# Retention's gates stored as products, with their silu in retention's stage, and attention's blocks begun less often in the first third of the gates

## The chip, the cores and the metric

The kernel runs on one core of one Trainium2 chip. The core has TensorE (PE in the profile, PEld for its weight loads), VectorE (DVE), ScalarE (ACT), GpSimd (POOL) and SyncE (SP), which here only issues transfers. Each engine takes its instructions in order from a queue of its own and waits on semaphores. The metric is the device time of one execution in microseconds, as the median of several runs. The time before is 2192.56 us, the median of three runs from 2191.86 to 2193.46.

## The reference

One decoder block on x of 1024 rows by 1024 columns, in float32. One input projection of the normalised rows feeds two mixers and the gates that merge them:

```
xn = rmsnorm(x, norm1_g)
qa, ka, va, qr, kr, vr, gr, gate_a, gate_b = columns of xn @ w_in
o_a = dilated sliding-window attention (12 heads, 3 dilations), mixed by softmax denominators
o_r = head_groupnorm(retention(qr, kr, vr)) * silu(gr)
y   = sigmoid(gate_a) * (o_a @ w_proj_a) + sigmoid(gate_b) * (o_r @ w_proj_b)
x   = x + y @ w_out
x   = x + square(relu(rmsnorm(x, norm2_g) @ w_up)) @ w_down
```

The change concerns `silu(gr)`, where silu(v) = v * sigmoid(v) and gr has 1024 rows by 2048 columns (4 heads of 512), and the time at which the pieces of attention are worked on.

## The kernel before

Every large product is done in three passes: each operand is split into a high and a low part (`split`, L369 on ScalarE and L372 on VectorE), and TensorE multiplies high by high, high by low and low by high (`Pipe.group`, L273). Weights come from memory into `raw` tiles, are split into `wh` and `wl` in six buffers, and are used (`Weights`).

TensorE's order is written out by hand. Its unit is a *slot* of `Pipe.step`: one group of matmuls, with other work put between the terms of the group if it is due in that slot (`Pipe.at(lag, ...)`). The order of the other engines and of the transfers is made by a planner, which goes by its own costs for instructions and transfers and gives earlier instructions of the program precedence; some orders are pinned (`keep_in_program_order`).

The stages that the change touches:

- **The gates' stage** (L871 on): 24 units of 7 slots, 168 slots, as a Strassen product (7 products of quarters instead of 8; `product`). Units 0 to 7 are the merge gates, `NG`; units 8 to 15 are retention's queries and keys, `NQ`; units 16 to 23 are retention's own gates `gr`. Each unit gives four results of 128x512: two come straight from PSUM (after N2 and N4), two from SBUF tiles `u2` and `u3` that VectorE has summed (L450, L455). `result` sends them out: the merge gates through a sigmoid (`gate_out`, L746, L747) into `sg_d`; queries and keys into `rqk_d`, copied first where they are in PSUM (L885); retention's gates through a sigmoid (L881) and a product with themselves (L882) into `sr_d`. The last two units' results go out on GpSimd's queue, the others on SyncE's (L886, L887). The pools `sg` and `u2`, `u3` have two buffers each.
- **Attention** runs in between: 96 blocks of 128 queries. Block n begins in slot `begins(n)` of this stage, with three pieces: `scores` in that slot (L814 on TensorE, L817 and L819 on VectorE, an exponential L820 on ScalarE), `turn` two slots later (L826 on TensorE, L828 on VectorE) and `values` four slots later (L833 on TensorE, a copy L835 on ScalarE, and for each second block a store). Each piece takes one of the two PSUM buffers `tr`. Loads of queries, keys and values (L786 to L788) are issued from SyncE ahead of the blocks.
- **The mix** of attention's three head groups, eight times (`combine`): loads 7 and 19 slots after the beginning of the last block of a head slot, arithmetic from 12 and 24 slots after it, with an exponential on ScalarE (L490), products on VectorE (L502, L504), transposes on TensorE (L510). Once the last block is done, `close_heads` frees attention's memory for more weight buffers.
- **Values for retention** (56 more slots of token units, L718 to L737), which still hold the last mix.
- **Retention** (L1129 on), over 32 items, a head and a chunk of 128 rows each, with the two output projections of the mixers as filler for TensorE. Item m is normalised (`output`), and two iterations later `turn_o` transposes it (L1118), scales and shifts it (L1122, Identity with a scale and a bias, four times 128x128 on ScalarE), multiplies it on VectorE by the gates in tile `sr` (L1124; loaded at L1030, two buffers) and splits it into the operand of a projection. Between them stand the splits of the state (`prepare`, tiles `Sh`, `Sl`).

Of the kernel before, what the change touches and what calls it, by code (L numbers as in the profile page):

```python
# [10 lines left out]
F = mybir.dt.float32  # L11
R = mybir.dt.float32r
AF = mybir.ActivationFunctionType
OP = mybir.AluOpType
PSUM = bass.MemoryType.PSUM
DRAM = bass.MemoryType.DRAM

P = 128
# [287 lines left out]
def strassen_order(units):  # L306


    order = [(0, "N1"), (1, "N1"), (0, "N2"), (1, "N2")]
    for j in range(units):  # L310
        late = j + 3 >= units
        order += [(j, "N6"), (j, "N5")] + ([] if late else [(j + 2, "N1")]) + [(j, "N7")]
        order += [(j, "N3")]
        order += [(j + 2, "N2")] if not late else [(units - 1, ("N1", "N2")[j + 3 - units])] if j + 1 < units else []
        order += [(j, "N4")]
    return order
# [3 lines left out]
def hybrid_block(ctx: ExitStack, tc: tile.TileContext, a: dict, out: bass.AP):  # L320
    nc = tc.nc
# [46 lines left out]
    def split(dst_h, dst_l, src, pinned=False):  # L368
        hi = nc.scalar.activation(dst_h, src, AF.Copy)  # L369
        if pinned:  # L370
            tc.keep_in_program_order(hi)
        nc.vector.tensor_tensor(dst_l, src, dst_h.bitcast(F), op=OP.subtract)  # L372
# [25 lines left out]
    NG, NQ = KT, 2 * RH  # L398
# [18 lines left out]
    pipe = Pipe(nc)  # L417

    def product(tag, j, name, unit, operands, pu, result):

        u = unit.setdefault(j, {})
        bank = BANK[name]
        fresh = bank not in u
        if fresh:
            u[bank] = mm.tile([P, 512], F, name="mm")
        piece, half = OPERAND[name]
        wh, wl = W[tag, j, piece]
        xh, xl = operands[name]
        terms = []
        for k in range(4):  # L430
            o = 512 * half + k * P
            terms.append((wh[:, o:o + P], wl[:, o:o + P], xh[:, k, :], xl[:, k, :]))
        pipe.step(u[bank], terms, None, fresh)
        ps = u[bank]
        lo, hi = halves()
        if name == "N1":
            u["b"] = ms.tile([P, 512], F, name="ms")
            nc.scalar.activation(u["b"], ps, AF.Copy, scale=-1.0)
        elif name == "N2":
            result(j, 0, lo, ps)  # L440
        elif name == "N6":
            u["u2"] = pu().tile([P, 512], F, name="u2")
            nc.scalar.activation(u["u2"], ps, AF.Copy)
        elif name == "N5":
            u["u3"] = pu().tile([P, 512], F, name="u3")
            nc.scalar.activation(u["u3"], ps, AF.Copy)
            if j == 0:
                W.free((tag, "first"))
        elif name == "N7":
            nc.vector.tensor_tensor(u["u3"], ps, u["u3"], op=OP.subtract)  # L450
            result(j, 1, hi, u["u3"])
        elif name == "N4":
            result(j, 1, lo, ps)
        elif name == "N3":
            nc.vector.tensor_tensor(u["u2"], ps, u["u2"], op=OP.subtract)  # L455
            result(j, 0, hi, u["u2"])
        if name in ("N2", "N7", "N4", "N3"):
            W.free((tag, j, piece))
# [58 lines left out]
    def mix_next():  # L517

        if mixing:
            mixing.pop(0)()  # L520
            if len(mixing) == 1:
                pipe.at(1, mixing.pop())
# [11 lines left out]
    def cut(t):  # L534
        return slice((t % 4) * P, (t % 4 + 1) * P)
# [208 lines left out]
    def gate_out(f, d, cs, src):  # L744
        sg = sgp.tile([P, 512], F, name="sg")
        nc.scalar.activation(sg, src, AF.Sigmoid)  # L746
        nc.sync.dma_start(sg_d[f, d, :, cs], sg)  # L747

    sgp = pu = att = cmb = dist = None
# [94 lines left out]
    load_pair(0)  # L844

    def begins(n):
        return 3 + (n * 19) // 12

    at_slot = {}
    for n in range(len(BLOCKS)):  # L850
        at_slot.setdefault(begins(n), []).append(lambda n=n: attend(n))
    joined = {}

    def close_heads():
        heads_.close()
        W.most = pool(tok, "most2", 1)
        W.pump()

    at_slot.setdefault(begins(len(BLOCKS) - 1) + 6, []).append(close_heads)

    def begin_mix(s, i):
# [3 lines left out]
    for s in range(SLOTS):  # L865
        e = begins(24 * s + 23) + 4
        for i in range(2):
            at_slot.setdefault(e + 3 + 12 * i, []).append(lambda s=s, i=i: joined.update({(s, i): load_heads(s, i, cmb)}))
            at_slot.setdefault(e + 8 + 12 * i, []).append(lambda s=s, i=i: begin_mix(s, i))

    with ExitStack() as ph:  # L871

        def result(j, f, cs, src):
            if j < NG:
                gate_out(f, j, cs, src)
                return
            n = j - NG
            sg = src
            if n >= NQ:
                sg = sgp.tile([P, 512], F, name="sg")  # L880
                nc.scalar.activation(sg, src, AF.Sigmoid)  # L881
                nc.vector.tensor_tensor(sg, src, sg, op=OP.mult)  # L882
            elif src.space == PSUM:
                sg = sgp.tile([P, 512], F, name="sg")
                nc.scalar.activation(sg, src, AF.Copy)  # L885
            queue = nc.gpsimd if n >= NQ + 6 else nc.sync  # L886
            queue.dma_start(sr_d[2 * (n - NQ) + f, :, cs] if n >= NQ else rqk_d[n // 2, n % 2, f, :, cs], sg)  # L887

        unit = {}
        step = iter(range(1000))  # L890

        def events():
            for fn in at_slot.pop(next(step), []):
                fn()
            mix_next()

        for j, name in strassen_order(NG + NQ + 8):
            events()
            product("in", j, name, unit, operands, lambda: pu, result)
# [43 lines left out]
    with ExitStack() as ph:  # L943
# [80 lines left out]
        state, its, srs = {}, {}, {}  # L1024
# [88 lines left out]

        def turn_o(m):
            h, c = ITEMS[m]
            pt = tr.tile([P, 4, P], F, name="tr")
            for f in range(4):
                nc.tensor.transpose(pt[:, f, :], its[m]["o"][:, f * P:(f + 1) * P], ident)  # L1118
            onT = p2.tile([P, 4, P], F, name="onT")
            for f in range(4):  # L1120
                fi = 4 * h + f
                nc.scalar.activation(onT[:, f], pt[:, f], AF.Identity, scale=gng[:, 0, fi:fi + 1],  # L1122
                                     bias=gng[:, 1, fi:fi + 1])
            nc.vector.tensor_tensor(onT, onT, srs.pop(m), op=OP.mult)  # L1124
            split(*(x[:, :, cut(c)] for x in (inner, before)[c // 4][h % 2]), onT)

        for m in range(len(ITEMS) + 3):
            acts = []
            if m >= 3:  # L1129
                acts.append(lambda m=m: turn_o(m - 3))  # L1130
            if m < len(ITEMS):
                load_item(m + 2)
                q, k = (ring[m % 4][:, 256 * i:256 * i + 256].rearrange("p (f t) -> p f t", f=2) for i in range(2))
                it = its[m] = {"raw": (q, k)}
                it["v"] = p2.tile([P, DV], R, name="vh", bufs=4), p2.tile([P, DV], R, name="vl", bufs=4)
                split(*it["v"], ring[m % 4][:, 512:])
                acts.append(lambda m=m: decay(m))
            if 2 <= m < len(ITEMS) + 2:
                load_sr(m - 2)
            if 1 <= m <= len(ITEMS):  # L1140
                acts += [lambda m=m: output(m - 1), lambda m=m: update(m - 1)]
            if m < len(ITEMS):
                acts.append(lambda m=m: prepare(m))
            if share[m] == 2:
                pipe.at(0, *acts[:2])
                pipe.at(1, *acts[2:])
            else:
                pipe.at(0, *acts)
            for _ in range(share[m]):
                fill.pop(0)()  # L1150
# [364 lines left out]
```

## Time and profile before

| | |
|---|---|
| median of three runs | 2192.56 us |
| profiled execution, time | 2193.37 us |
| profiled execution, span from first to last instruction | 2191.6 us |
| TensorE busy | 2153.8 us, 98% |
| VectorE busy | 1487.0 us, 68% |
| ScalarE busy | 1139.9 us, 52% |
| GpSimd busy | 170.0 us, 8% |
| gates' stage with retention's gates' last result | about 404 to 957 us |
| retention's items | about 1120 to 1420 us |

The span is that of one profiled execution; the time of that execution is 1.8 us longer, and the median of the other runs lies 0.8 us below it. A busy share is an average over stages that have different limits, so the stages are read one by one. In a line of waits stand the waiting engine, its tile and line, then what it waited for, the total in us, how often, and the longest. In a group of instructions stand line, engine, operation, output<-inputs, shapes, count, then busy us and mean ns of one, then the idle time of the engine just before them and what ended it. In a line of the order of time stand start and duration in us. An ACT_TABLE_LOAD is the instruction with which ScalarE changes its table of functions.

### The profile page before, as it was taken

To read this page: it belongs to the slowest core of one execution; us is meant where nothing else is said; L and a number is where in the kernel's file an instruction comes from. 1 tells how busy PE (TensorE), PEld (TensorE's weight loads), DVE (VectorE), ACT (ScalarE), POOL (GpSimd) and SP (SyncE) were. 2 spreads that over 40 slices of the span, in tenths; PEclk is the share of its full clock that TensorE was granted. 3 is DMA by queue.
4 is the path that set the end of the run, shared out by engine and by line. 5 is a ranking of instruction groups with operands and counts; after the bars stand their busy time and mean duration, and the time that the engine had idled before them with its cause. 6 is when DMAs were issued, how large, how long until landed. Compare 5 with 4: busy or idle time off the path is not lost.

```text
span 2191.6 us, 28596 instructions
## 1 busy us (share of the span) xinstructions
PE 2153.8 (98%) x9968; PEld 1769.8 (81%) x9968; DVE 1487.0 (68%) x2627; ACT 1139.9 (52%) x1990; POOL 170.0 (8%) x183
## 2 busy tenths in 40 slices
PE   8999999999999999999999999999999999999998
PEld 6888788888788887788888888888788888778887
DVE  8767676455555657676579778665788878587764
ACT  6434443567844567842246666533577777532210
POOL 1114353000000000000000000100000000000002
PEclk9999999999999999999999999999999999999999
DMA  5433434544545545454577555664388889885758
GB/s 204 130 116 103 147 97 121 159 144 149 169 147 167 170 148 163 134 189 140 173 238 235 180 158 180 180 234 134 103 251 247 247 247 290 305 288 223 261 211 178
DMA packets 335972, 403.29 MB, mean 184 GB/s; under 512 B 35346, under 2 KB 252050, under 8 KB 335827
## 3 DMA queue, kind: packets, MB, share of 16 engines
q1 hardware_dynamic: 331490, 392.28, 56.5%
q0 software_dynamic: 4336, 9.18, 2.3%
q8 instruction: 79, 1.29, 0.2%
q14 instruction: 67, 0.54, 0.1%
HBM read 262.87 MB, written 138.51 MB: 183 GB/s over the span
## 4 chain that ended last, share of the span: by engine, by line
PE 55%; issue 30%; DVE 6%; ACT 3%; DMA 3%; POOL 1%; SPq 0%; POOLq 0%; ACTq 0%; DVEq 0%
PE mm L273 28%; PE ms L273 22%; PE tr L814 1%; DVE wl L372 1%; PE tr L833 1%; PE tr L665 1%; ACT wh L369 1%; DMA sg_d<-sg 1%; PE ms L1041 1%; PE tr L826 1%; DMA sr_d<-sg 1%; DVE xl L372 1%; DVE raw L159 1%; POOL out L1357 1%; PE tr L1118 0%
## 5 line engine op out<-in xcount | busy, mean ns | idle before, releaser
L369 ACT ACTIVATE wh<-raw 128x1024 fp32r<-128x1024 f32 (+1 forms) x319 | 316.1, 993 | 309.2 <-PE ms L273 181.9
L372 DVE TENSOR_TENSOR wl<-raw,wh 128x1024 fp32r<-128x1024 f32 (+1 forms) x319 | 366.1, 1152 | 142.4 <-ACT wh L369 137.7
L273 PE MATMUL mm<-xh,wh 128*128 128x512 f32 x960 | 397.9, 415 | 0.0
L273 PE MATMUL mm<-xh,wl 128*128 128x512 f32 x960 | 376.3, 392 | 0.0
L273 PE MATMUL mm<-xl,wh 128*128 128x512 f32 x960 | 375.6, 391 | 0.3 <-DVE xl L372 0.3
L273 PEld LDWEIGHTS mm<-xh,wl 128*128 128x128 f32 x960 | 180.1, 188 | 39.7
L273 PEld LDWEIGHTS mm<-xh,wh 128*128 128x128 f32 x960 | 181.3, 189 | 32.5
L273 PEld LDWEIGHTS mm<-xl,wh 128*128 128x128 f32 x960 | 181.3, 189 | 31.2 <-DVE xl L372 0.9
L273 PE MATMUL mm<-wh,xh 128*128 128x512 f32 x520 | 205.7, 396 | 0.0
L273 PE MATMUL mm<-wh,xl 128*128 128x512 f32 x520 | 203.3, 391 | 2.1 <-DMA xl<-h_d 2.1
L273 PE MATMUL ms<-xh,wh 128*128 128x512 f32 x480 | 201.2, 419 | 3.1 <-ACT xh L369 2.5
L273 PE MATMUL mm<-wl,xh 128*128 128x512 f32 x520 | 202.7, 390 | 0.0
L273 PE MATMUL ms<-wh,xh 128*128 128x512 f32 x504 | 202.2, 401 | 0.3 <-ACT wh L369 0.3
L273 PE MATMUL ms<-wl,xh 128*128 128x512 f32 x504 | 197.3, 391 | 1.6 <-DVE wl L372 0.8
L273 PE MATMUL ms<-wh,xl 128*128 128x512 f32 x504 | 197.5, 392 | 0.0
L273 PE MATMUL ms<-xl,wh 128*128 128x512 f32 x480 | 188.4, 393 | 0.7 <-DVE xl L372 0.7
L273 PE MATMUL ms<-xh,wl 128*128 128x512 f32 x480 | 188.7, 393 | 0.0
L273 PEld LDWEIGHTS mm<-wh,xl 128*128 128x128 f32 x520 | 97.7, 188 | 23.2 <-DMA xl<-h_d 2.5
L273 PEld LDWEIGHTS mm<-wl,xh 128*128 128x128 f32 x520 | 97.9, 188 | 19.3
L273 PEld LDWEIGHTS mm<-wh,xh 128*128 128x128 f32 x520 | 97.8, 188 | 19.4 <-ACT ms L1346 0.4
L273 PEld LDWEIGHTS ms<-wl,xh 128*128 128x128 f32 x504 | 95.5, 190 | 21.0 <-DVE wl L372 2.3
L273 PEld LDWEIGHTS ms<-wh,xl 128*128 128x128 f32 x504 | 95.3, 189 | 20.8
(326 smaller groups left out, 3838.3 us busy)
## 6 DMA issues: line engine op xcount, KB each, us to landing
h_d<-hs SPq DMA_DIRECT2D x112, 512.0 KB, 4.1
xh<-h_d SPq DMA_DIRECT2D x32, 896.0 KB, 5.3
xl<-h_d SPq DMA_DIRECT2D x32, 896.0 KB, 7.4
raw<-in_w_att_q SPq DMA_DIRECT2D x48, 512.0 KB, 4.5
raw<-in_w_up SPq DMA_DIRECT2D x32, 512.0 KB, 3.7
raw<-in_w_pb SPq DMA_DIRECT2D x32, 512.0 KB, 4.2
raw<-in_w_down SPq DMA_DIRECT2D x32, 512.0 KB, 4.8
qk_d<-T SPq DMA_DIRECT2D x48, 256.0 KB, 3.4
```

The source lines that it names most:

```text
L159: self.nc.vector.tensor_tensor(x, x, y, op=OP.add)
L273: self.nc.tensor.matmul(ps, x, y, start=start, stop=stop, skip_group_check=not first)
L369: hi = nc.scalar.activation(dst_h, src, AF.Copy)
L372: nc.vector.tensor_tensor(dst_l, src, dst_h.bitcast(F), op=OP.subtract)
L665: nc.tensor.transpose(pt[:, i, :], c[:, i * P:(i + 1) * P], ident)
L814: nc.tensor.matmul(sp[:, :w], q[:, e * P:(e + 1) * P], k[:, k0 * P:k0 * P + w], start=True, stop=True)
L826: nc.tensor.transpose(tb[:, j * P:(j + 1) * P], st["p"][:, j * P:(j + 1) * P], ident)
L833: nc.tensor.matmul(po[:, :DH], st["t"][:, j * P:(j + 1) * P], v[:, k0 + j, :], start=(j == 0), stop=(j == nk - 1))
L1041: nc.tensor.matmul(sp[:, i * P:(i + 1) * P], key[:, f], q[:, f], start=(f == 0), stop=(f == 1))
L1357: nc.gpsimd.dma_start(out[r * P:(r + 1) * P, ns], Y[r][:, ns], accum_op=OP.add)
```

## The change

Retention's gates are stored without their silu. In units 16 to 23 the sigmoid and the product go; a result in PSUM is copied out, as for queries and keys, and one in SBUF is stored from its tile. In retention, `turn_o` first puts the tile `sr` through ScalarE's Silu, in place, and the product then takes that. Both the number and the size of the stores and loads stay.

The beginnings of attention's blocks move: the first 27 blocks begin every second slot, at 3 to 55, where 19 slots held 12 blocks before; the others follow at 10 slots for 7 blocks, from 57 on. The last begins in slot 154 instead of 153. The mixes and `close_heads`, whose slots are reckoned from `begins`, move along: the four head slots' last blocks begin in slots 49, 85, 119 and 154, where it was 39, 77, 115 and 153.

```diff
     def begins(n):
-        return 3 + (n * 19) // 12
+        return 3 + 2 * n if n < 27 else 57 + ((n - 27) * 10) // 7
...
             n = j - NG
             sg = src
-            if n >= NQ:
-                sg = sgp.tile([P, 512], F, name="sg")
-                nc.scalar.activation(sg, src, AF.Sigmoid)
-                nc.vector.tensor_tensor(sg, src, sg, op=OP.mult)
-            elif src.space == PSUM:
+            if src.space == PSUM:
                 sg = sgp.tile([P, 512], F, name="sg")
                 nc.scalar.activation(sg, src, AF.Copy)
             queue = nc.gpsimd if n >= NQ + 6 else nc.sync
...
         def turn_o(m):
             h, c = ITEMS[m]
+            sr = srs.pop(m)
+            nc.scalar.activation(sr, sr, AF.Silu)
             pt = tr.tile([P, 4, P], F, name="tr")
...
-            nc.vector.tensor_tensor(onT, onT, srs.pop(m), op=OP.mult)
+            nc.vector.tensor_tensor(onT, onT, sr, op=OP.mult)
             split(*(x[:, :, cut(c)] for x in (inner, before)[c // 4][h % 2]), onT)
```

## The prediction

> **What bounds the kernel now.** I read the page first, then the busy times by stretch, then the waits and the ScalarE groups of each stretch, and last the order of time around single stops. The page's head:
>
> ```profile
> span 2191.6 us, 28596 instructions
> PE 2153.8 (98%) x9968; PEld 1769.8 (81%) x9968; DVE 1487.0 (68%) x2627; ACT 1139.9 (52%) x1990; POOL 170.0 (8%) x183
> ```
>
> TensorE is the bound, and the change takes no matmul from it. So the change is worth what TensorE's stops are worth in the stretches that it touches, and no more. The stretches are the eight gate units (404 to 600 us), the eight units of retention's queries and keys (600 to 755), retention's own gates (755 to 957, attention ending near 926) and retention itself (1120 to 1420); the last line is a stretch of plain matmuls for comparison. Behind the bounds stand the length and each engine's busy time with its count (TensorE, its weight loads, VectorE, ScalarE, GpSimd):
>
> ```profile
> 404.00:600.00 196.00, 194.28 (x942) 159.28 (x941) 102.65 (x262) 148.70 (x248) 0.00 (x0) 1.00 0.50 153
> 600.00:755.00 155.00, 154.16 (x757) 127.47 (x756) 91.23 (x269) 68.33 (x155) 0.00 (x0) 1.00 0.54 166
> 755.00:926.00 171.00, 167.26 (x814) 136.40 (x812) 107.04 (x272) 126.58 (x211) 0.77 (x1) 1.00 0.46 146
> 1120.00:1205.00 85.00, 84.36 (x416) 69.38 (x415) 77.43 (x170) 52.77 (x115) 6.69 (x10) 1.00 0.79 249
> 1205.00:1420.00 215.00, 215.00 (x1049) 178.60 (x1048) 163.83 (x335) 139.31 (x285) 22.14 (x30) 1.00 0.58 173
> ...
> 1650.00:1700.00 50.00, 50.00 (x223) 41.39 (x222) 40.79 (x57) 36.10 (x59) 0.00 (x0) 1.00 0.91 255
> ```
>
> ScalarE is busy 76% in the first stretch and 74% in the third, but 44% in the second, which runs the same attention blocks at the same pace. The difference is table loads. These are all that there are, by line, and then attention's own (L820) in the first, second and third stretch, the third up to 957:
>
> ```profile
> L820 ACT ACT_TABLE_LOAD x40 | 51.3, 1283 | 6.0 <-DVE acc L819 3.5 <-issue 1.7
> L746 ACT ACT_TABLE_LOAD x23 | 29.5, 1283 | 5.2 <-DMA sg_d<-sg 3.6 <-issue 1.2
> L881 ACT ACT_TABLE_LOAD x21 | 26.9, 1283 | 3.4 <-DMA sr_d<-sg 3.1
> L490 ACT ACT_TABLE_LOAD x4 | 5.1, 1283 | 0.1
> L590 ACT ACT_TABLE_LOAD x1 | 1.3, 1283 | 0.7 <-PEq L1505 0.7
> ```
> ```profile
> L820 ACT ACT_TABLE_LOAD x21 | 26.9, 1283 | 4.0 <-DVE acc L819 3.5 <-issue 0.3
> ```
> ```profile
> L820 ACT ACT_TABLE_LOAD x1 | 1.3, 1283 | 0.0
> ```
> ```profile
> L820 ACT ACT_TABLE_LOAD x18 | 23.1, 1283 | 2.0 <-issue 1.5
> ```
>
> Sigmoid (L746 in the gate units, L881 in retention's gates) and Exp (L820, and L490 in the mix) evict each other's table. TensorE's waits, in the same three stretches:
>
> ```profile
> PE tr L814 <- ACT acc L835: 0.9, 1, 0.9
> PE tr L826 <- ACT acc L835: 0.5, 1, 0.5
> PE tr L814 <- DVE pT L828: 0.2, 1, 0.2
> ```
> ```profile
> PE tr L510 <- DVE edge L504: 0.8, 1, 0.8
> ```
> ```profile
> PE tr L826 <- ACT s L820: 2.0, 3, 1.0
> PE tr L826 <- ACT acc L835: 0.8, 1, 0.8
> PE ms L273 <- ACT u L443: 0.6, 1, 0.6
> PE tr L814 <- ACT acc L835: 0.2, 1, 0.2
> ```
>
> The reader is to see that ScalarE stops TensorE only where loads are. One stop, in order of time, shows how:
>
> ```profile
> 851.36 0.38 PE L833 MATMUL tr<-v,pT 128*128 128x128 f32 x2
> 853.59 1.28 ACT L881 ACT_TABLE_LOAD   x1 [2.28 <-DMA sr_d<-sg]
> 855.38 0.27 ACT L835 ACTIVATE acc<-tr 128x128 f32<-128x128 f32 x1
> 855.71 0.49 PE L814 MATMUL tr<-k,q 128*128 128x128 f32 x2 [0.17 <-ACT acc L835]
> ```
>
> The values matmuls (L833) fill a bank of `tr` at 851.4; ScalarE empties it only at 855.4, behind a sigmoid that waited for its buffer's store and then for its table. The scores (L814) need that bank, as `tr` has two.
>
> A stop costs more than its idle time. Matmuls are booked as 0.391 us long, yet follow each other every 50/223 = 0.224 us, so each stop costs 0.167 us on top:
>
> ```profile
> L273 PE MATMUL mm<-xl,wh 128*128 128x512 f32 x960 | 375.6, 391 | 0.3 <-DVE xl L372 0.3
> ```
>
> **Retention's gates (755 to 957).** The edit removes 32 sigmoids, 21 + 18 loads of 1.283 us, and 32 products, half of them these:
>
> ```profile
> L882 DVE TENSOR_TENSOR sg<-u,sg 128x512 f32<-128x512 f32 x16 | 11.0, 686 | 2.6 <-ACT sg L881 2.6
> ```
>
> Sixteen results are copied out of PSUM instead (0.58 us, as L885 does; its row is below), and sixteen are stored straight from `u`. The stores stay 24 on SP's and 8 on POOL's queue. A `u` buffer is used again two units (14 slots of about 3.3 us: 404 to 957 us hold 168) later, so no store is waited for. What runs here afterwards is, in kind, what runs from 600 to 755, and there ScalarE stopped TensorE not once. The stops are 2.0 + 0.8 + 0.6 + 0.2 = 3.6 us in 6 stops, with 6 x 0.167 that is 4.6. The pace gives a second reading: 757 matmuls took 155 - 0.8 - 0.2 = 154.0 us in the stretch before, 0.2034 each, so the 814 up to 926 would take 165.6 of their 171: 5.4 us lost. I take the middle, **5.0 us gained**. Bounds: 0, if other work takes the stops' place, and 5.4.
>
> **Gate units (404 to 600).** The stops there are 0.9 + 0.5 + 0.2 = 1.6 us in 3, with 3 x 0.167 2.1 us. By the formula for the beginnings, 34 blocks began in slots 0 to 55 and 27 will. A unit's four results fall in four consecutive slots and exponentials in every second one, which makes two runs of sigmoids per unit: four loads, an estimate of 32 instead of the 45 (23 + 21 of the rows, and one of L490). Slot 0's mix, with its own load, moves from slot 51 to 61, out of the sigmoids. So these stops should mostly go: **2.1 us gained**.
>
> But the new spacing has a price of its own. A block's scores, turn and values run 0, 2 and 4 slots after its beginning. With beginnings every second slot all three meet in one slot, 25 times instead of 5, and then scores take the bank that values left two steps earlier. The one stop of the five such slots:
>
> ```profile
> 469.66 0.38 PE L833 MATMUL tr<-v,pT 128*128 128x128 f32 x2
> 469.60 1.28 ACT L746 ACT_TABLE_LOAD   x1
> 471.43 0.26 ACT L835 ACTIVATE acc<-tr 128x128 f32<-128x128 f32 x1
> 471.71 0.49 PE L814 MATMUL tr<-k,q 128*128 128x128 f32 x2 [0.16 <-DVE pT L828]
> ```
>
> The wait for the bank (emptied by L835 at 471.69) and for L828's data ended together. That is 0.16 + 0.17 = 0.33 us in five, 0.066 per meeting, times 25 = 1.65; with 32 loads for 45 I take **1.2 us lost**. Bounds: 0, and 25 x 0.33 = 8.2 if each meeting stops.
>
> **Later blocks.** From slot 57 on a block begins every 1.43 slots instead of 1.58, ending one slot later; close_heads and the last mix follow by one. The blocks bring their loads on SP with them, spread over the same queue. With ScalarE at 44% in the stretch that shows this without loads, I cost it at nothing; were that cover gone, a meeting would cost 0.33 us, and there are 21 against 10. The mix's 0.8 us stop (L510) hangs on VectorE and stays.
>
> **Retention (1120 to 1420).** 32 Silus on 128x512 in SBUF are added and one load of 1.28. No Silu is in the trace; the nearest row is the sigmoid from SBUF, the lower neighbour the copy from PSUM:
>
> ```profile
> L881 ACT ACTIVATE sg<-u 128x512 f32<-128x512 f32 x16 | 10.1, 631 | 3.0 <-DVE u L455 2.6 <-DVE u L450 0.2
> ```
> ```profile
> L885 ACT ACTIVATE sg<-ms 128x512 f32<-128x512 f32 x6 | 3.5, 581 | 0.0
> ```
>
> I take the first, whose operand lies where Silu's will. So 32 x 0.63 = 20.2 us of ScalarE, 23 of them (14.5 us) where it is idle 215 - 139.3 = 75.7 us. The narrow place is before 1205, where VectorE is busy 77.4 of 85 us:
>
> ```profile
> PE ms L273 <- DVE Sl L372: 0.6, 2, 0.4
> ```
> ```profile
> L369 ACT ACTIVATE xh<-onT 128x512 fp32r<-128x512 f32 x9 | 5.7, 630 | 14.1 <-DVE onT L1124 14.1
> ```
> ```profile
> DMA to landing us min/median/max: 2.7/4.2/6.4
> ```
>
> The last line is that of the `sr` tiles' loads. Nine Silus come here, as nine operands do: 9 x 0.63 + 1.3 = 7.0 us, the upper bound of the loss. The lower is 0: ScalarE waits 14.1 us for VectorE's product with the gates, 1.6 per operand, so a Silu fits there; and with two `sr` buffers a load can start once the product two items before is done, and lands within 6.4 us. Behind a Silu in the queue stand the four scalings, the copies of the state and the next operand; of these only the state has no slack (its low half made TensorE wait 0.6 us). I take **0.5 us lost**, near the lower bound because of the 14.1.
>
> **Sum.** -5.0 - 2.1 + 1.2 + 0.5 = -5.4 us, on the profiled execution's 2193.37 us: 2188.0. The median of the runs, 2192.56, lies 0.8 below it, so 2187.2 is predicted for a median. About 0.2% (4.4 us) is what a measurement of this kernel can tell from no change: 2188.2 is the bound.
>
> **Rivals.** (A) the sum, chance 0.70, own range 2185 to 2189.4; 0.50 of the 0.70 lies under the bound. (B) The meetings decide: half of the 25 stop for 0.33 us, 4.1 us instead of 1.2: 2190.1. For it: 469.60, a load just as values ran. Against: four of five meetings without a stop. Chance 0.11. (C) No gain: ScalarE loses its loads but the stops pass to VectorE, 63% busy from 755 to 926, whose own stop at L510 is not touched: between 0 and 2 us gained, 2191.5. Against: the middle stretch. Chance 0.09. (D) Slower: before 1205 the Silu is put ahead of the state's copies before its data has landed, and ScalarE stands there. Price 0.63 + (4.2 - 2.7) = 2.1 us per item; the 5.9 us gained before retention are gone from the third item on; six items and the load are 14 us, so 2192.6 - 5.9 + 14 = 2200.7. For it: no slack at the state's low half. Against: 14.1 us of idle ScalarE, and loads issued early. Chance 0.07. (E) Silu's table lacks the scaling's function: loads at both, 64 x 1.28 = 82 us on top of 20 and the 52.8 + 139.3 of now, 294 of 300 us; where a tenth of the added 102 us reaches TensorE, 10 us, which gives 2192.6 - 5.9 + 10 = 2196.7. Against it: by the five groups of loads above, no copy and no scaling ever loaded, whichever table was in. The Trainium skill, "ScalarE: Activation LUTs", section "Table sets: the hidden batching unit", says the same, that cheap functions such as copy and identity are in every set; by that rule E cannot be, and for the two sets used here the trace agrees; for Silu's set no run here shows it yet. Chance 0.03.
>
> **How the numbers follow.** Faster: 0.50, from A. Within 0.2%: 0.20 of A, B and C, 0.40. Slower: D and E, 0.10. The range runs from 2184.5 (both stretches' stops gone at no price, 7.5 gained by the pace, and half a microsecond below it) to 2192.2, which takes in B and C.
>
> **What would show it.** Right: loads down from 89 (40 + 23 + 21 + 4 + 1) to some 35, none from 755 on but one at Silu; no wait of TensorE for ScalarE in retention's gates; ScalarE near 45% there. Wrong: several L814 stops behind L835 in the gate units (B); stops at L814 or L826 released by VectorE (C); waits for the state before 1205 of over 2 us, with ScalarE waiting for the load of `sr` (D); a load beside each L1122 (E).

## The result, and the profile after

The changed kernel took **2201.63 us** in the median of 22 runs, against 2191.75 us of the kernel before beside it: the ratio is 1.0046 (95% interval 1.0038 to 1.0055), so it is about 10 us slower. 2187.2 us had been predicted, with 0.10 for slower. The single runs lie further apart than the first three of the kernel before did: its 22 runs went from 2186.6 to 2199.0 us, those of the changed one from 2193.5 to 2211.9. Times below are medians of many runs; stages are read from one profiled execution of each kernel. The profiled execution of the changed kernel took 2204.54 us.

The page of the changed kernel begins with the span and each engine's busy time:

```profile
span 2202.7 us, 28445 instructions
PE 2156.8 (98%) x9968; PEld 1770.5 (80%) x9968; DVE 1464.8 (67%) x2595; ACT 1084.9 (49%) x1961; POOL 166.9 (8%) x183
```

VectorE has 22 us less to do and ScalarE 55 us less; TensorE has the same matmuls; and the span is 11.1 us longer. Neither engine became a bound, then, and the question is where TensorE stood.

Three rows cut the span into stages: the copy of the first gate unit (L438), the transposes of retention's items (L1118, now L1116), and those of the second norm (L1197, now L1195). The last two numbers before the shapes are the first and last start. First the kernel before, then the changed one:

```profile
L438 ACT ACTIVATE ms<-mm x40: 573/581/588, 402.9 to 1836.9; 128x512 f32<-128x512 f32 x40
L1118 PE MATMUL tr<-ident,on x128: 270/273/273, 1129.5 to 1415.3; 128*128 128x128 f32 x128
L1197 PE MATMUL tr<-ident,xn x60: 270/272/328, 1517.7 to 1564.3; 128*128 128x128 f32 x60
```
```profile
L438 ACT ACTIVATE ms<-mm x40: 575/580/582, 403.6 to 1846.1; 128x512 f32<-128x512 f32 x40
L1116 PE MATMUL tr<-ident,on x128: 270/272/273, 1125.3 to 1417.6; 128*128 128x128 f32 x128
L1195 PE MATMUL tr<-ident,xn x60: 270/272/328, 1528.2 to 1574.8; 128*128 128x128 f32 x60
```

From 402.9 to 1129.5 are 726.6 us and from 403.6 to 1125.3 are 721.7: the gates and the values for retention **gained 4.9 us**. From 1129.5 to 1517.7 are 388.2 us and from 1125.3 to 1528.2 are 402.9: retention **lost 14.7 us**. What lies before and after these stages adds 1.3 us.

**The gates' stage did about what was meant.** The busy times by stretch of the changed kernel, in two of the stretches shown of before, and the 20 us behind retention's last item:

```profile
404.00:600.00 196.00, 192.27 (x916) 157.37 (x915) 96.09 (x218) 142.76 (x228) 0.00 (x0) 1.00 0.48 145
...
755.00:926.00 171.00, 170.79 (x846) 141.32 (x845) 101.98 (x291) 75.30 (x174) 0.77 (x1) 1.00 0.49 155
...
1420.00:1440.00 20.00, 15.22 (x53) 11.69 (x54) 9.48 (x12) 9.75 (x19) 1.73 (x2) 0.83 0.81 233
```

From 755 to 926 ScalarE is busy 75.3 us instead of 126.6, and TensorE 170.8 of the 171 us instead of 167.3. From 404 to 600 it is busy for less, 192.3 instead of 194.3. The table loads, by line, and TensorE's waits from 395 to 980 us:

```profile
L746 ACT ACT_TABLE_LOAD x21 | 26.9, 1283 | 3.9 <-DMA sg_d<-sg 2.4 <-issue 1.2
L820 ACT ACT_TABLE_LOAD x21 | 26.9, 1283 | 0.4
L590 ACT ACT_TABLE_LOAD x1 | 1.3, 1283 | 0.7 <-PEq L1503 0.7
L1113 ACT ACT_TABLE_LOAD x1 | 1.3, 1283 | 0.0
```
```profile
PE tr L814 <- ACT acc L835: 3.7, 4, 1.1
PE tr L814 <- DVE mx L817: 0.2, 1, 0.2
```

89 loads became 44. Retention's 32 Silus have one between them (L1113), and there is none at the scalings. What is left of TensorE's waits for ScalarE stands where values and scores meet: four stops, all in the gate units, each with the load of a sigmoid's table (L746) ahead of the copy L835.

**Retention is where the time went.** ScalarE's wait for the loads of `sr`, from 1120 to 1430 us; then, from the view of the tile `sr`, the issues of its loads (with the first and last start), the Silus, and the time that a load took:

```profile
ACT sr L1113 <- DMA sr<-sr_d: 79.5, 28, 6.5
```
```profile
L1026 SPq DMA_DIRECT2D sr<-sr_d x32: 370/371/518, 1118.4 to 1414.6; - x32
L1113 ACT ACTIVATE sr<-sr x32: 630/632/649, 1122.8 to 1418.6; 128x512 f32<-128x512 f32 x32
...
DMA to landing us min/median/max: 2.9/4.2/6.9
```

A Silu takes 0.632 us, as was put for it. But 28 of the 32 stood at the head of ScalarE's queue before their data was there, 79.5 us in all. Most of this was covered, as the starts of the transposes (L1118, now L1116) tell. Items 8 to 23 take 154.2 us in both kernels, though the waits for their `sr` sum to 37.7 us. Items 0 to 7, with 9.4 us of waits, take 2.1 us longer, items 24 to 31, with 32.5 us of waits, 4.4, and from the last item's transposes to those of the norm it is 8.2 us longer. The last four waits:

```profile
ACT sr L1113 <- DMA sr<-sr_d: 20.1, 4, 6.5
```

This is the same wait from 1380 to 1430 us, and these are the instructions around two of them, in order of time (start, duration; in brackets the idle time ahead and what ended it):

```profile
1386.95 0.37 SPq L1026 DMA_DIRECT2D sr<-sr_d  x1
1387.80 0.58 ACT L1077 ACTIVATE on<-ms 128x512 f32<-128x512 f32 x1
1393.91 0.63 ACT L1113 ACTIVATE sr<-sr 128x512 f32<-128x512 f32 x1 [5.53 <-DMA sr<-sr_d]
1394.44 1.13 ACT L369 ACTIVATE Sh<-St 128x512 fp32r<-128x512 f32 x2
1395.11 0.49 PE L273 MATMUL ms<-Sh,qh 128*128 128x512 f32 x1 [0.92 <-ACT Sh L369]
...
1418.63 0.63 ACT L1113 ACTIVATE sr<-sr 128x512 f32<-128x512 f32 x1 [6.46 <-DMA sr<-sr_d]
1426.32 0.64 ACT L369 ACTIVATE xh<-onT 128x512 fp32r<-128x512 f32 x1
1427.01 0.79 PE L273 MATMUL mm<-xh,wh 128*128 128x512 f32 x1 [3.23 <-ACT xh L369]
1428.61 0.79 PE L273 MATMUL mm<-xl,wh 128*128 128x512 f32 x1 [0.81 <-DVE xl L372]
1429.20 0.63 PE L273 MATMUL mm<-xh,wl 128*128 128x512 f32 x1
1429.63 0.63 PE L273 MATMUL mm<-xh,wh 128*128 128x512 f32 x1
```

The load is issued at 1386.95. ScalarE reaches the Silu at 1388.38, as its instruction before ends, and stands for 5.53 us until the data lands. Behind it stand the copies of the state (`Sh`), and TensorE waits 0.92 us for them. The last Silu is held for 6.46 us: ScalarE reaches it 2.4 us before its load, the last of the 32, is even issued at 1414.6, and the load takes another 4.1. The scalings and the operand `xh` of the last items come after it, and at 1427.01 TensorE has stood 3.23 us for that operand. No item follows, whose matmuls could have filled the gap. All of TensorE's waits from 1120 to 1450 us in the changed kernel, where the kernel before had two, of 0.6 us together:

```profile
PE mm L273 <- ACT xh L369: 3.2, 1, 3.2
PE ms L273 <- DVE Sl L372: 2.3, 6, 0.6
PE ms L273 <- ACT Sh L369: 1.5, 2, 0.9
PE mm L273 <- ACT mm L1001: 0.8, 1, 0.8
PE mm L273 <- DVE xl L372: 0.8, 1, 0.8
PE ms L273 <- DVE edge L1039: 0.7, 1, 0.7
```

They add up to 9.3 us in 12 stops, 11.3 with 0.167 for each restart; 14.7 were lost. The rest is in the last two lines of the order of time: after the stop, matmuls follow each other every 0.43 us instead of 0.224. The stretch from 1420 to 1440 shows the granted clock at 0.83 in the mean, and 53 matmuls; the kernel before has 1.00 and 89 there:

```profile
1420.00:1440.00 20.00, 20.00 (x89) 16.41 (x88) 12.94 (x18) 9.91 (x15) 0.00 (x0) 1.00 0.93 308
```

The 36 that are missing are 36 x 0.224 = 8.1 us: the stops around the hand-over to plain projections, with the slower pace behind them, are over half of the loss.

### The profile page after: what moved, and what is told of

Its sections match the earlier page's. It is cut to its first block, busy times and chain, and to the rows that moved or that the text cites. A ratio compares the mean times of both kernels' runs of the same rounds, so it can differ in the third digit from the quotient of the medians.

```text
span 2202.7 us, 28445 instructions
## 1 busy us (share of the span) xinstructions
PE 2156.8 (98%) x9968; PEld 1770.5 (80%) x9968; DVE 1464.8 (67%) x2595; ACT 1084.9 (49%) x1961; POOL 166.9 (8%) x183
## 4 chain that ended last, share of the span: by engine, by line
PE 58%; issue 30%; DVE 5%; DMA 4%; ACT 2%; POOL 1%; SPq 1%; POOLq 0%; ACTq 0%; DVEq 0%
PE mm L273 29%; PE ms L273 23%; PE tr L814 1%; PE tr L833 1%; DMA sr<-sr_d 1%; PE tr L665 1%; DMA pa_d<-s 1%; PE tr L826 1%; DVE xl L372 1%; DVE wl L372 1%; POOL out L1355 1%; PE ms L1037 0%; ACT wh L369 0%; PE tr L1116 0%; DMA ring<-rv_d 0%
```

## The experiments

All times are medians; the ratio is to the kernel before in the same series, with its 95% interval. It is not the quotient of the two medians (for late_old_begins that would be 0.9985).

| run | median us (runs) | kernel before | ratio |
|---|---|---|---|
| late | 2187.09 (11) | 2191.45 | 0.9983 (0.9975 to 0.9992) |
| silu_only | 2199.21 (11) | 2191.45 | 1.0030 (1.0019 to 1.0041) |
| begins_only | 2188.05 (11) | 2191.45 | 0.9987 (0.9978 to 0.9996) |
| no_silu | 2184.08 (7) | 2191.45 | 0.9967 (0.9955 to 0.9979) |
| wait_only | 2191.33 (11) | 2190.80 | 1.0002 (0.9993 to 1.0011) |
| late_twice | 2188.67 (10) | 2190.80 | 0.9991 (0.9979 to 1.0002) |
| late_old_begins | 2187.54 (11) | 2190.80 | 0.9977 (0.9965 to 0.9989) |
| next_old_begins | 2186.24 (11) | 2190.80 | 0.9979 (0.9971 to 0.9988) |
| late_tail | 2189.66 (12) | 2190.44 | 0.9999 (0.9990 to 1.0008) |
| late_lag5 | 2185.16 (5) | 2190.44 | 0.9970 (0.9958 to 0.9982) |
| next_lag5 | 2186.29 (12) | 2190.44 | 0.9976 (0.9967 to 0.9986) |

And the two stages of each one's profile, from the first copy of a gate unit to the first transpose of an item, and from there to the first transpose of the second norm, as worked out above for two of them. In the last two columns, the wait for `sr` on ScalarE, and the longest stop of TensorE at the hand-over to plain projections. What lies outside these two stages is the same work in all kernels, and takes between 1071.8 and 1078.1 us in these profiles; so the span of a single profile is no measure of a change.

| run | gates and values, us | retention, us | wait for sr, us | hand-over stop, us |
|---|---|---|---|---|
| before | 726.6 | 388.2 | none | none |
| after | 721.7 | 402.9 | 79.5 | 3.2 |
| late | 720.3 | 389.3 | none | none |
| silu_only | 720.4 | 400.5 | 75.9 | 2.9 |
| begins_only | 724.0 | 388.2 | none | none |
| no_silu | 719.6 | 388.4 | none | none |
| wait_only | 719.3 | 395.3 | 59.3 | 2.2 |
| late_twice | 721.0 | 392.5 | none | 0.8 |
| late_old_begins | 720.3 | 391.8 | none | none |
| next_old_begins | 719.2 | 391.6 | under 1 | none |
| late_tail | 720.0 | 391.5 | 47.9 | none |
| late_lag5 | 719.2 | 391.8 | none | none |
| next_lag5 | 718.8 | 389.5 | under 1 | none |

### The Silu moved behind the scalings (late)

```diff
         def turn_o(m):
             h, c = ITEMS[m]
             sr = srs.pop(m)
-            nc.scalar.activation(sr, sr, AF.Silu)
...
                                      bias=gng[:, 1, fi:fi + 1])
+            tc.keep_in_program_order(nc.scalar.activation(sr, sr, AF.Silu))
             nc.vector.tensor_tensor(onT, onT, sr, op=OP.mult)
```

> The whole change, but each Silu is pinned behind the four scalings of the same item, so that it stands behind them in ScalarE's queue and its load has had an item more to land. Theory W (the loss is the wait: a Silu stands in the queue before its load has landed, and the copies of the state behind it are late): ScalarE's wait for the load of sr falls from 79.5 us to under 5, TensorE's stops from 1350 to 1430 us go, the clock stays full there, and the time is 2185 to 2189, some 4 us under the kernel before. Theory B (the loss is the added work, 20 us of Silu and a table load, wherever it stands): 2197 to 2202, TensorE still stops in retention.

It took 2187.09 us, 14.5 less than the changed kernel, with the same 32 Silus. Two groups of its order of time show why: the issues of two `sr` loads, and the Silus that use them.

```profile
1385.53 0.39 SPq L1026 DMA_DIRECT2D sr<-sr_d  x1
1397.92 0.39 SPq L1026 DMA_DIRECT2D sr<-sr_d  x1
```
```profile
1403.64 0.64 ACT L1121 ACTIVATE sr<-sr 128x512 f32<-128x512 f32 x1
1409.58 0.64 ACT L1121 ACTIVATE sr<-sr 128x512 f32<-128x512 f32 x1
```

The last load is issued at 1397.92 and the last Silu runs at 1409.58, 11.7 us later, where the changed kernel's first one shown above stood ready 1.4 us after the issue. There is one Silu to a load, in the same order, so the one at 1403.64 belongs to the load of 1385.53, 18.1 us before. ScalarE never waits for `sr`, and these are all of TensorE's waits from 980 to 1480 us:

```profile
PE ms L273 <- DVE edge L1039: 0.7, 1, 0.7
PE ms L273 <- DVE Sl L372: 0.4, 1, 0.4
```

What took its place is harmless: VectorE's product now waits for the Silu, 17.1 us in 18 times, and TensorE for none of it. The clock stays at 1.00, and the 20 us of the hand-over hold 90 matmuls instead of 53:

```profile
1420.00:1440.00 20.00, 20.00 (x90) 16.53 (x89) 14.84 (x22) 11.21 (x18) 0.00 (x0) 1.00 0.91 305
```

So the place of the Silu in the queue is what made the changed kernel slow. This run alone does not say whether standing there or working there costs the time, nor what each half of the change is worth.

### The gates' part alone (silu_only), and without the Silu (no_silu)

```diff
# silu_only: the changed kernel, with
-        return 3 + 2 * n if n < 27 else 57 + ((n - 27) * 10) // 7
+        return 3 + (n * 19) // 12
# no_silu: besides
-            nc.scalar.activation(sr, sr, AF.Silu)
```

> The change with the beginnings of attention's blocks as they were before. Theory W and theory B: the loss in retention is all there, and the gain of retention's gates (about 5 us) too, so 2198 to 2204, near the changed kernel. Theory M (the loss is that of the new beginnings, through the slots where values and scores meet): 2186 to 2189.

> Retention's gates stored as products and old beginnings, and no Silu at all: the output lacks the silu of retention's gates, so this times what the removal in the gates' stage is worth by itself. Theories W, B: TensorE's stops from 755 to 957 us (4.6 to 5.4 us) go and nothing comes back in retention: 2185 to 2188. If the removal is worth nothing there, as a rival of the prediction had it: 2190 to 2193.

With the old beginnings the loss is still there: 2199.21 us, retention 12.1 us longer than without the Silu (400.5 against 388.4), with the same two signs as in the changed kernel: ScalarE waits 75.9 us for `sr`, and TensorE stops for 2.9 us at the hand-over. And what the gates' stage gains is in the stretch from 755 to 926 us of silu_only, with blocks begun as before:

```profile
755.00:926.00 171.00, 171.00 (x839) 141.98 (x839) 98.92 (x251) 73.89 (x162) 1.33 (x2) 1.00 0.50 154
```

TensorE is never idle there, and does 839 matmuls instead of 814. Without the Silu, retention takes 388.4 us, as before (388.2). So the new beginnings have no part in the loss. And no_silu gives the price of what the gates' stage was rid of: 7.4 us in the median, 7.0 in the stage (719.6 against 726.6), more than the 2185 to 2188 that were expected.

### The new beginnings alone (begins_only)

```diff
-        return 3 + (n * 19) // 12
+        return 3 + 2 * n if n < 27 else 57 + ((n - 27) * 10) // 7
```

> The kernel before with the new beginnings alone; the sigmoids and products in the gates' stage stay. Theories W and B: retention is as before, the gates' units gain what leaves them and lose what the meetings cost, retention's gates keep their table loads; 2190 to 2194, no change that can be measured. Theory M: 2198 or more.

It took 2188.05 us, 3.4 less than before, 2.6 of it in the gates' stage, where no measurable change had been expected. But on top of the other half the new beginnings are worth nothing: late takes 2187.09 and 720.3 us in the stage, and the same with the old beginnings (late_old_begins, below) 2187.54 and 720.3. TensorE's waits from 395 to 980 us in begins_only:

```profile
PE tr L814 <- ACT acc L835: 3.5, 4, 1.1
PE tr L814 <- DVE pT L828: 0.9, 1, 0.9
PE tr L826 <- ACT acc L835: 0.4, 1, 0.4
```

The 3.5 us all lie in the gate units, where the kernel before had 1.6: there the new beginnings cost. From 600 to 980 us it had 4.8 us, and 1.3 are left: that is what they bring. Most of those stops stood among the sigmoids of retention's gates, and the other half of the change takes them away by itself. So the two halves of the change save the same stops: in late_old_begins 2.5 us of waits are left from 395 to 980, in late, with the new beginnings, 2.7, all in the gate units:

```profile
PE tr L814 <- ACT acc L835: 2.7, 4, 1.1
```

This is read from the stops; no run separates the gain of the new beginnings from their price.

### The wait without the work (wait_only)

```diff
# silu_only, with
-            nc.scalar.activation(sr, sr, AF.Silu)
+            nc.scalar.activation(sr[:, 0, 0:1], sr[:, 0, 0:1], AF.Copy)
```

> Old beginnings; in the place of each Silu stands a copy of a single column of sr onto itself: it waits for the load as the Silu does, with hardly any work and no table load. The output lacks the silu. Theory W: ScalarE still waits 60 to 80 us for the load of sr, TensorE still stops at the end of retention, and the time is 2193 to 2198, near the kernel with unpinned Silus and old beginnings (2199.2) and some 10 us over the kernel with no Silu (2184.1). Theory B: 2184 to 2186, as with no Silu.

A copy of one column has little work, 0.20 us against 0.63, but must wait for the load as the Silu does. 2191.33 us, below the range expected by theory W and far above that of theory B, is 7.3 more than no_silu, which differs from it by this copy alone; retention is 6.9 us longer, 1.5 of it in items 0 to 7 and 5.4 behind the last item. ScalarE's wait, TensorE's stop at the hand-over, and the 20 us around that stop:

```profile
ACT sr L1113 <- DMA sr<-sr_d: 59.3, 27, 6.2
```
```profile
PE mm L273 <- ACT xh L369: 2.2, 1, 2.2
```
```profile
1410.00:1430.00 20.00, 16.68 (x65) 13.08 (x65) 11.27 (x17) 9.69 (x17) 1.73 (x2) 0.91 0.89 279
```

So standing in the queue costs some 7 us, the copies' 6.5 us of work included, and again the clock falls behind the stop: 65 matmuls, where late has 88 in the same 20 us.

### The work without the wait, twice (late_twice), and once with the old beginnings (late_old_begins)

```diff
# late_twice: late, with the pinned line a second time
+            tc.keep_in_program_order(nc.scalar.activation(sr, sr, AF.Silu))
# late_old_begins: late, with
+        return 3 + (n * 19) // 12
```

> The change with each Silu pinned behind the scalings (2187.1), and a second Silu on the same tile behind it, so that ScalarE has 32 x 0.63 = 20 us more to do; the output has silu twice. Theory W: work that does not wait is covered, so 2187 to 2191. Theory B: another step like the first, 2196 or more.

> Each Silu pinned behind the scalings, old beginnings. Theory W says nothing of the beginnings; with the new ones this was 2187.1. If the beginnings are worth what they gave alone (3.4 us): 2189 to 2191. If they only help where the table loads of retention's gates are, and cost by their meetings else: 2184 to 2187.

Twenty more microseconds of ScalarE's work, where nothing waits for a load, cost some 1.6 us: 2188.67 against 2187.09, with intervals that overlap, and 3.3 by the retention stage of the one profile. The first 20 us of work can be priced with the old beginnings, where a kernel without the Silu exists: 3.4 us in the stage (391.8 against 388.4) and 3.5 in the median, though from two series, and the intervals of their ratios overlap too. By the starts of the transposes, 3.1 of these 3.4 us and 2.2 of the 3.3 lie in items 0 to 7; with the new beginnings the same 20 us of work (late) cost only 0.6 us there. So 20 us of work that doesn't wait cost between 0.9 us (late against no_silu, in the stage) and 3.4, most of it in the first items. 2187.54 us lies just above the lower of the two ranges that were expected for the old beginnings.

Wait and work together cost more than the two apart: 12.1 us in retention (silu_only) against 6.9 and 3.4. The excess of about 2 us shows in the last items: items 24 to 31 take 3.4 us longer in silu_only than in no_silu, but 0.0 us longer in wait_only and late_old_begins. Why is not settled.

### The Silu one item ahead (next_old_begins, next_lag5)

```diff
# old beginnings; next_lag5: the new ones, and values five slots after the beginning
+        def silu(m):
+            if m in srs:
+                tc.keep_in_program_order(nc.scalar.activation(srs[m], srs[m], AF.Silu))
         def turn_o(m):
+            if m == 0:
+                silu(0)
             h, c = ITEMS[m]
             sr = srs.pop(m)
-            nc.scalar.activation(sr, sr, AF.Silu)
...
             split(*(x[:, :, cut(c)] for x in (inner, before)[c // 4][h % 2]), onT)
+            silu(m + 1)
```

> Old beginnings; the Silu of the next item is pinned behind this item's split, an item ahead of its product, when its load was issued a whole item before. Theory W: no wait for the load (under 5 us), and the scalings no longer stand before it on the way to the product: retention as with no Silu within 0.5 us, 2184 to 2186. Theory B: 2194 or more.

> As the run before, with each Silu an item ahead of its product, behind the split of the item before. Candidate for the best version: 2182 to 2186, no wait of ScalarE for the load of sr over 1 us after the first item.

The next item's Silu behind the item's own split also leaves the load its time, and frees VectorE's product from waiting. 2186.24 and 2186.29 us: as good as late, and no better beyond the intervals; both lie just above the ranges expected. Retention was expected within 0.5 us of the kernel without the Silu, and takes 391.6 us in next_old_begins against 388.4, again longer in the first items. So it matters that the Silu stands well after the load; where it stands behind that matters little.

### Only the last eight items pinned (late_tail)

```diff
             sr = srs.pop(m)
-            nc.scalar.activation(sr, sr, AF.Silu)
+            if m < 24:
+                nc.scalar.activation(sr, sr, AF.Silu)
...
+            if m >= 24:
+                tc.keep_in_program_order(nc.scalar.activation(sr, sr, AF.Silu))
```

> The change with only the last eight Silus (items 24 to 31) pinned behind the scalings; the first 24 are left where the planner puts them, and wait for their loads as before. Theory W in its narrower form (the 2 to 4 us waits of items 0 to 27 are mostly covered, those of the last items, 4 to 7 us, are not): ScalarE still waits some 50 us for the load of sr, but retention takes 389 to 391 us from its first to the hand-over instead of 402.9, and the time is 2187 to 2191. If every wait counted alike, three quarters of the loss would stay: 2196 to 2199.

Nineteen waits remain, and the stop at the hand-over is gone. ScalarE's wait, and TensorE's waits from 1120 to 1450 us:

```profile
ACT sr L1114 <- DMA sr<-sr_d: 47.9, 19, 4.4
```
```profile
PE ms L273 <- DVE Sl L372: 1.9, 4, 0.7
PE ms L273 <- DVE edge L1039: 1.1, 1, 1.1
```

Retention takes 391.5 us: of the 13.6 us between the changed kernel and late, the pins on the last eight items alone give back 11.4, though 47.9 of the 79.5 us of waiting are still there. How much of the remaining 2.2 the waits of the first 24 items cost isn't told: 1.3 of it lies in items 0 to 7, whose time varies as much between kernels that never wait, and 1.0 in items 16 to 23. In medians it is 2189.66 against 2187.09, each beside its own series of the kernel before: 0.0016 of the ratio, 3.5 us, with intervals that just overlap.

### Values five slots after the beginning (late_lag5)

```diff
# late, with
-        pipe.at(4, values)
+        pipe.at(5, values)
```

> The change with each Silu pinned behind the scalings (2187.1), and attention's values five slots after a block's beginning instead of four, so that with beginnings every second slot they no longer meet the scores in one slot. If the meetings are what the new beginnings cost in the gate units: TensorE's waits at L814 for L835 fall from 2.7 us in 4 to under 0.7, and the time is 2183 to 2186. If they aren't: 2186 to 2189, with stops elsewhere.

It takes the scores and the values of two blocks apart where beginnings come every second slot. Of the stops behind L835, two of the four are left, 1.5 us where under 0.7 had been expected, so the meeting in one slot isn't all of their cause:

```profile
PE tr L814 <- ACT acc L835: 1.5, 2, 0.8
```

2185.16 us is the lowest median of a kernel with the whole output, 0.9970 of the kernel before, but on five runs, and its interval overlaps those of late, late_old_begins, next_lag5 and next_old_begins. Any of the five beats the kernel before and the changed one; which is best isn't told apart.

## Why the prediction was wrong

It was wrong by its sign and by 14.4 us, and its range ended at 2192.2. Step by step:

**What bounds the kernel** was right: TensorE does, and what was found of the loss is stops of TensorE, and its clock behind one of them.

**Retention's gates, 5.0 us gained.** The mechanism was right: with the old beginnings 755 to 926 us go from 814 to 839 matmuls, and 25 x 171/839 is 5.1 us. The whole part is worth more, 7.0 us in the stage by no_silu, and 6.2 by silu_only. The term was too small by 1 to 2 us; it stopped at the stretch that was read. "No wait of TensorE for ScalarE there" held. Rival C fell: the stops did not pass to VectorE.

**The gate units, 2.1 us gained, and the meetings, 1.2 lost.** Net 0.9 was put for the beginnings. In the gate units it came out the other way: the stops there went from 1.6 us in 3, 2.1 with 0.167 for each, to 2.7 in 4 (late), 3.4 with 0.167 for each. The table loads in that part were put at 32 and were 21 + 21 = 42, against 45, and in the changed kernel each of the four stops stands behind a load. So the meetings' price was too low: 1.2 us were put, 3.4 came. That is near rival B's 4.1, though in four stops of 0.7 us and not in twelve of 0.33. What the beginnings gave alone, 3.4 us in the median, came later, at stops that the other half takes away too. The mix's stop at L510, which was to stay, is gone with the new beginnings. Beside the other half, the beginnings so brought 0.9 us less than was put, which about cancels the error above.

**Retention, 0.5 us lost: this is the step that failed.** It rests on one sentence: "ScalarE waits 14.1 us for VectorE's product with the gates, 1.6 per operand, so a Silu fits there; and with two `sr` buffers a load can start once the product two items before is done, and lands within 6.4 us." The second half was right: in the changed kernel, too, a load is issued once the product two items before is done, in most items at once, and lands within 6.9 us. But nothing in the sum priced what happens if the Silu gets to the head of the queue sooner than that; the upper bound, 7.0 us, is work alone. The queue was ordered by the planner, and nothing bound the Silu to a place: in the program it came ahead of the transposes, with its tile's load as its only input, and in ScalarE's queue it came ahead of the copies of the state and of the scalings. By the order of time, the 32 Silus got to the head of the queue 1.6 us after the issue of their load in the median, where landing takes 4.2: hence 79.5 us of waits, and 14.7 us lost in retention, of which 1.1 are lost in late too.

The first half, that a Silu fits into the 14.1 us, doesn't hold as it stands either. In that gap ScalarE waits for the product of an item, and the product needs the Silu of the same item, so only another item's could stand there. In the changed kernel 7.5 of the 14.1 us are left before 1205, and in late the product waits 17.1 us for the Silu.

With each Silu pinned behind the scalings, the sum came near: -5.4 us was predicted and late took -4.4 (-3.7 by the ratio). That is partly luck: the gates gave 1 to 2 us more than was put, the beginnings 0.9 less, and the Silu's work cost 0.9 us (late against no_silu in retention) to 3.4 (late_old_begins) instead of 0.5.

**Rival D** named this: the Silu ahead of the state's copies, its data not landed, at 0.07. The size even agrees, 14 us put and 14.7 lost, but by accident. It placed the loss before 1205 us, where VectorE is full, in six items at 2.1 us. There, ScalarE waited 11.2 us in 7 times, and TensorE's first eight items took 2.1 us longer, 0.8 of it also in late. The loss sits at the other end, in the last items, 4.4 us from item 24 to item 31 and 8.2 behind. The rival asked where an engine is narrow, and not where the cover ends: at the last item nothing follows that TensorE could do while it waits. Its argument against, "loads issued early", was not checked against the order of the queues; and "14.1 us of idle ScalarE" is no argument against a wait that is put into the queue.

**Rival E** fell: one load for 32 Silus, and none at the scalings between them.

**What was left open.** The first eight items take from 67.3 to 70.6 us in these kernels: 67.3 to 67.5 in those without a wait for `sr` and without a Silu, but 68.0 to 70.6 in those with pinned Silus, which wait for `sr` at most once; there TensorE waits for VectorE's copies of `edge` (L1039), up to 1.8 us at a time. This moves late against late_old_begins by 2.5 us in the retention stage, and why is not known. Nor is why wait and work together cost more than the sum. And that the planner's own idea of a load's duration sets the Silu's place is only argued, from 28 waits out of 32; no run changed it.

## What to carry to other kernels

An instruction that needs only a load, moved into a stage with a full queue, can be put at a place that the engine reaches before the load has landed, and then everything behind it on that engine waits too; so its price may be not its duration but its place, and that has to be pinned behind work that is later than the load for sure (here one line, worth 14.5 us). Idle time on an engine shows that work can fit, not that it will be put there. Look at the last items of a pipelined loop first: here 37.7 us of waits in items 8 to 23 cost nothing, while the last items, and the hand-over behind them, lost 12.6 us.

## What the runs showed of the hardware

**A short stop costs more than itself.** Behind the 3.23 us stop matmuls ran 0.43 us apart until about 1433.5, then 0.23 again, and 20 us held 53 instead of 89: 8.1 us for waits of 3.23, 0.81 and 0.82. Two more kernels show it, at a granted clock below 1 in the 20 us around the stop (1410 to 1430): wait_only with 2.2 us (0.91) and silu_only with 2.9 (0.83). No kernel without such a stop shows it there; late_twice, with stops of 0.8 and 0.2 us, has 1.00. The Trainium skill, "TensorE: Matmul & The Clock Gate", section "What's actually happening", has the array at half clock after an idle window of about 3.4 us, which runs freely. The Trainium skill, "TensorE: Matmul & The Clock Gate", section "Wait — 56ns, not 53.3ns?", puts matmuls of 512 columns 426.7 ns apart on that clock; the 0.43 us agree. But the stops here are shorter, 2.2 to 3.2 us, or 2.4 to 3.4 with 0.167 for the end as booked; if a whole window has to be without any matmul, the rule would have spared at least the shorter ones. In all three kernels a second stop, of 0.8 to 1.1 us, follows one matmul later; whether the first alone would have been enough, no run shows. Such a stop has to be priced with the half-speed matmuls behind it, here some 3 us more (8.1 less the 4.9 us of waits).
